# Query parts stored unsplit, key/value weights taken up later, and norm steps issued further on

## The chip, the core and the metric

The kernel runs on one core of one Trainium2 chip. The metric is the device time of one execution in microseconds (us): a median over runs, here 2845.11 us of 3 runs (2842.18 to 2846.28). Five engines work side by side, each through its own list of instructions in order: PE multiplies matrices and writes to PSUM (8 banks here, one tile `ps` each), DVE (VectorE) and ACT (ScalarE) do elementwise work, POOL (GpSimd) does some more of it, and SP issues nearly all DMA transfers. An instruction that waits holds up all that stands behind it on its engine.

## The reference, cut to what matters

One step of a diffusion backbone with two layers and 1152 tokens (1024 latent ones, 128 of context), 1024 features wide. Layer 0 mixes tokens with a gated recurrence, layer 1 with latent attention; each is followed by an MLP with a hidden width of 4096, and every sublayer starts with an RMS norm whose result is scaled and shifted by values worked out from a conditioning vector.

```python
for l in range(DEPTH):
    sh1, sc1, g1, sh2, sc2, g2 = adaln_params(c, ada_w[l], ada_b[l])
    h = modulate(rms_norm(xs, norm_mix[l]), sh1, sc1)
    if l % N_MIXERS == 0:
        out, _ = rglru_block(h, ...)
    else:
        q_nope, q_pe, ckv, kpe = mla_project(h, ...)     # 8 heads, 128 + 64 query rows each
        q_pe = apply_rope(q_pe, ...)
        k_nope, v = mla_kv(ckv, w_ukv)                   # keys, values of each head
        out = block_attention(q_nope, q_pe, k_nope, kpe, v) @ mla_w_o[j]
    xs = xs + g1[:, None, :] * out
    h = modulate(rms_norm(xs, norm_mlp[l]), sh2, sc2)
    xs = xs + g2[:, None, :] * sq_relu_mlp(h, mlp_w1[l], mlp_w2[l])
y_sample = rms_norm(xs, final_norm)
```

## The kernel before, in words

**Layout.** Features lie on the 128 partitions, tokens along the free axis, in three chunks of 384 tokens (`c` = 0, 1, 2; the last has 256 latent and 128 context tokens, so its elementwise steps come in pairs of 256 and 128). A product of 1024 features is 8 blocks of 128, for each of which `mm3` issues three matmuls of 384 columns, since each operand is held as a rounded high part and the low rest (`hi`, `lo`): hi·hi, hi·lo, lo·hi (L120, L123, L124). `split` (L138, L139) makes the two parts: an ACT cast writes `hi`, a DVE subtraction writes `lo`.

**Weights.** They come as a stream of 181 pieces of 128x1024. `prefetch` issues each one's DMA to `raw` (two buffers), an ACT cast to `whi` (L93) and a subtraction to `wlo` (L95, on POOL for all but the first pieces). `done(i)` says that piece i is used up and takes up the pieces three or four further on. With each piece, `prefetch` also issues `ada_rate` rows of the weights that make layer 1's scales and shifts: a DMA (L152) and two DVE dot products of 1024 elements (L144).

**Products and drains.** `group` goes through the chunks and in each through the output tiles m; after the matmuls of a tile it calls `drain`, which reads the PSUM bank. In `out_proj` (after the token mixer) and in the last of the eight groups of `mlp`, the drain adds the scaled product to the residual `X` (L297, DVE), and `sq_acc` squares the row on ACT (L221, L225) and adds the square to one of two sums per chunk (L227): even rows on DVE, odd rows on POOL.

**Norms.** When a chunk's last tile is out, `group` puts the generator `norm_mod(c)` on a list. After each tile `tick` takes 0.49 per block off its countdown, and when it is used up the generator goes on to its next `yield`. So `yield 2.9` means: one tile of 8 blocks (24 matmuls) further on, or two tiles of 4 blocks. The first part, `rstd`, sums over the partitions with six small matmuls against ones (L235, they wait for both sums) and works out the inverse root in 12 DVE steps on 128x3 values, `sv`, `st` and `sy` (L242 to L256). The second part, `spread`, transposes `sy` on PE (L263), and `modulate` makes the next products' operands `hhi`, `hlo` from it, 8 rows of 384 with a DVE, an ACT and a DVE step each (L283, L287, L288).

**Queries.** In `mla`, `qnope` splits each finished query tile from PSUM into `qn` and stores both parts to the DRAM tensor `qn_d` (L853), four heads at a time: 12 stores of 768 KB. The rotary parts `qpe` go through DMA swaps (L719, L720) and are stored to `qp_d` (L840). `attention` then loads three tiles of 576 KB per head (L882), makes values and keys of the first heads (`gen_v`, L909 to L911; `gen_k`) and starts on the scores. Before it the pools of `mla` are released, so tiles of `attention` lie where the query tiles lay and wait for these to be stored.

**Order.** The order in the code isn't the order on the engines: when the kernel is built, a scheduler takes the instructions of each stretch of code and orders each engine's list by its own model. Only instructions marked with `keep_in_program_order` keep their place.

## Time and profile before

| | |
|---|---|
| median of 3 runs | 2845.11 us (2842.18 to 2846.28) |
| the profiled execution | 2843.63 us, its span 2841.9 us |
| busy: PE, DVE, ACT, POOL | 97%, 49%, 41%, 17% of the span |
| granted TensorE clock, mean | 0.987 of full speed |
| gate outputs of `out_proj` and norms after the recurrence | about 440 to 512 us |
| last MLP group of layer 0 and its norms | about 1255 to 1335 us |
| queries, first values and keys | about 1400 to 1514 us |
| attention | 1514 to 1960 us |
| norms after the attention's `out_proj` | about 1975 to 2040 us |

The 40 slices of the page show PE at nine tenths or more nearly everywhere. So the views to read are PE's waits in a stretch of time (engine, line, what was waited for: sum in us, times, longest), and the busy time by stretches, with the granted clock (PEclk).

### The profile page before, as it was taken

How to read it: one execution, taken by the hardware profiler on the slowest of the kernel's cores; microseconds unless marked ns; L12 is line 12 of the kernel's file. 1: busy time of each engine (PE TensorE's matmuls, PEld its weight loads, DVE VectorE, ACT ScalarE, POOL GpSimd, SP SyncE). 2: the span in 40 equal slices, each digit the busy share in tenths (PEclk: the TensorE clock that was granted, in tenths of full speed). 3: DMA queues.
4: the chain of work that ended last, by engine and by line, in shares of the span. 5: the costliest groups of instructions: out<-in, count | busy, mean ns of one | idle time of the engine just before them, and what ended most of it. 6: DMA issues, size and time to landing. Idle time of an engine off the chain costs nothing. (4 is left out here: it accounts for less than half of the span.)

```text
span 2841.9 us, 39879 instructions
## 1 busy us (share of the span) xinstructions
PE 2749.7 (97%) x16123; PEld 2679.4 (94%) x16123; DVE 1403.4 (49%) x2806; ACT 1158.3 (41%) x2194; POOL 483.1 (17%) x247
## 2 busy tenths in 40 slices
PE   6999998999999999998998999999999999999998
PEld 3878898999999999998997999999999999999998
DVE  7788967545444542245545666652632222223225
ACT  4677733331232233144336777762422312322232
POOL 1000033121121212122241000002221211212121
PEclk9999999999999999999998999999999999999999
DMA  6122242222232221112264121134010111101011
GB/s 254 45 89 93 71 180 72 67 82 97 67 104 67 92 80 45 45 52 90 66 196 171 48 82 59 54 113 148 30 60 30 52 38 38 52 30 60 30 45 67
DMA packets 79465, 224.93 MB, mean 79 GB/s; under 512 B 7856, under 2 KB 36336, under 8 KB 77616
## 3 DMA queue, kind: packets, MB, share of 16 engines
q1 hardware_dynamic: 78512, 219.23, 22.6%
q0 software_dynamic: 768, 3.15, 0.3%
q8 instruction: 127, 2.08, 0.3%
q14 instruction: 58, 0.48, 0.1%
HBM read 186.52 MB, written 33.20 MB: 77 GB/s over the span
## 5 line engine op out<-in xcount | busy, mean ns | idle before, releaser
L95 POOL TENSOR_TENSOR wlo<-raw,whi 128x1024 fp32r<-128x1024 f32 x161 | 396.1, 2461 | 2009.0 <-ACT whi L93 1976.9
L120 PE MATMUL ps<-hhi,whi 128*128 128x384 f32 x2088 | 701.9, 338 | 3.6 <-ACT hhi L287 3.6
L123 PE MATMUL ps<-hlo,whi 128*128 128x384 f32 x2088 | 703.2, 337 | 0.0
L124 PE MATMUL ps<-hhi,wlo 128*128 128x384 f32 x2088 | 702.5, 337 | 0.4 <-DVE wlo L95 0.4
L93 ACT CAST whi<-raw 128x1024 fp32r<-128x1024 f32 x181 | 190.3, 1052 | 875.7 <-PE ps L123 729.8
L297 DVE SCALAR_TENSOR_TENSOR X<-ps,mod,X 128x256 f32<-128x256 f32 (+1 forms) x576 | 281.2, 513 | 493.5 <-PE ps L124 453.6
L120 PE MATMUL ps<-hid,whi 128*128 128x384 f32 x1536 | 516.3, 336 | 0.0
L123 PE MATMUL ps<-hid,whi 128*128 128x384 f32 x1536 | 515.5, 336 | 0.0
L124 PE MATMUL ps<-hid,wlo 128*128 128x384 f32 x1536 | 515.4, 336 | 0.0
L120 PEld LDWEIGHTS ps<-hhi,whi 128*128 128x128 f32 x2088 | 393.8, 189 | 12.1 <-ACT hhi L287 4.0
L123 PEld LDWEIGHTS ps<-hlo,whi 128*128 128x128 f32 x2088 | 394.2, 189 | 5.6 <-issue 5.2
L124 PEld LDWEIGHTS ps<-hhi,wlo 128*128 128x128 f32 x2088 | 394.2, 189 | 1.0 <-DVE wlo L95 1.0
L139 DVE TENSOR_TENSOR hid<-cell,hid 128x384 fp32r<-128x384 f32 x192 | 141.7, 742 | 491.7 <-ACT hid L138 491.6
L120 PEld LDWEIGHTS ps<-hid,whi 128*128 128x128 f32 x1536 | 288.9, 188 | 0.0
L123 PEld LDWEIGHTS ps<-hid,whi 128*128 128x128 f32 x1536 | 288.8, 188 | 0.0
L124 PEld LDWEIGHTS ps<-hid,wlo 128*128 128x128 f32 x1536 | 288.7, 188 | 0.0
L352 ACT ACTIVATE cell<-ps 128x384 f32<-128x384 f32 x192 | 93.6, 489 | 305.6 <-PE ps L124 305.6
L144 DVE SCALAR_TENSOR_TENSOR junk<-raw,cb 128x1024 bf16<-128x1024 f32 x56 | 99.7, 1781 | 106.7 <-DMA raw<-ada_wt 106.7
L947 ACT ACTIVATE p<-ps,nm 128x384 f32<-128x384 f32 (+1 forms) x200 | 112.9, 577 | 38.0 <-DVE nm L942 38.0
L139 DVE TENSOR_TENSOR pt<-ps,pt 128x384 fp32r<-128x384 f32 (+1 forms) x200 | 106.5, 543 | 36.8 <-ACT pt L138 36.5
L932 DVE TENSOR_REDUCE mx<-ps 128x1 f32<-128x384 f32 (+1 forms) x200 | 107.9, 539 | 25.7 <-PE ps L931 25.0
L353 ACT ACTIVATE cell<-cell 128x384 f32<-128x384 f32 x192 | 100.6, 525 | 5.9
(188 smaller groups left out, 4084.6 us busy)
## 6 DMA issues: line engine op xcount, KB each, us to landing
raw<-wts SPq DMA_DIRECT2D x181, 512.0 KB, 3.3
raw<-ada_wt SPq DMA_DIRECT2D x56, 512.0 KB, 3.3
adaw<-ada_n SPq DMA_DIRECT2D x24, 512.0 KB, 4.1
qn_d<-qn SPq DMA_DIRECT2D x12, 768.0 KB, 5.3
q<-qn_d SPq DMA_DIRECT2D x16, 576.0 KB, 5.2
o_d<-o SPq DMA_DIRECT2D x64, 128.0 KB, 1.7
x<-xt SPq DMA_DIRECT2D x3, 1536.0 KB, 14.1
X<-xt SPq DMA_DIRECT2D x3, 1536.0 KB, 11.8
```

Source lines behind the costliest of these rows:

```text
L93: nc.scalar.copy(out=hi, in_=raw)
L95: eng.tensor_tensor(out=lo, in0=raw, in1=hi.bitcast(F32), op=ALU.subtract)
L120: mm = nc.tensor.matmul(ps, lhsT=w[0], rhs=h[0], start=first, stop=False)
L123: nc.tensor.matmul(ps, lhsT=w[0], rhs=h[1], start=False, stop=False)
L124: nc.tensor.matmul(ps, lhsT=w[1], rhs=h[0], start=False, stop=last)
L139: (lo_eng or nc.vector).tensor_tensor(out=lo, in0=src, in1=hi.bitcast(F32), op=ALU.subtract)
L144: self.nc.vector.scalar_tensor_tensor(out=w if cond else self.junk, in0=w, scalar=1.0, in1=self.cb[cond], op0=ALU.mult, op1=ALU.mult, accu ...
L297: self.nc.vector.scalar_tensor_tensor(out=self.X[c][:, m, a:b], in0=ps[:, a:b], scalar=self.mod[:, l, j, cond, m:m + 1], in1=self.X[c][:, ...
L352: nc.scalar.activation(out=r, in_=ps, func=AF.Relu)
L353: nc.scalar.activation(out=r, in_=r, func=AF.Square)
L932: nc.vector.tensor_reduce(out=mx[:, j:j + 1], in_=ps, axis=AX.X, op=ALU.max)
L947: nc.scalar.activation(out=p[:, j * CH:j * CH + w], in_=ps, func=AF.Exp, scale=SCALE, bias=nm[:, 1:2], accum_out=sm[:, j:j + 1],)
```

## The change

1. **Norms.** In `norm_mod` the two countdowns become 4.0 and 5.0 (2.9 each before). For tiles of 8 blocks that is two tiles and two more; for tiles of 4 blocks three and three more. The final norm (`after` in `second_half`) keeps 2.9 and 2.9.
2. **Sums of squares.** Of the odd rows, the last one (i = 7) is added on DVE, not on POOL.
3. **Conditioning rows.** In `out_proj` the rate at which these rows are taken along with weights is set after the second `dense`, not before it.
4. **Queries.** `qnope` copies each tile from PSUM unsplit (one DVE copy); 6 stores of 768 KB take the place of 12. `attention` loads the unsplit tile into one new buffer `qraw` (two loads a head in place of three) and splits it into the `hi` and `lo` tiles there, a chunk of 384 at a time: for the first head after the first values and keys, for the others in steps 3 to 5 of the head before.
5. **Weights.** From the start of the query products, `prefetch` stops (`cap`) at the second of the four key/value pieces; the stop is lifted once the first values and keys and the first head's query parts are issued.

```diff
--- before.py
+++ after.py
@@ -61,6 +61,7 @@
         self.pending = []
         self.wpx = None
         self.pin = False
+        self.cap = 1 << 30
         self.ready = []
         self.used, self.oldest = set(), 0
         self.ada_i = 0
@@ -83,7 +84,7 @@
         nc = self.nc
         if self.wpx is None:
             upto = min(upto, len(RG_STREAM) + 3)
-        while self.piece_i < min(upto, self.I["wts"].shape[0]):
+        while self.piece_i < min(upto, self.cap, self.I["wts"].shape[0]):
             raw = self.wp.tile([128, 1024], F32, tag="raw", name="raw", bufs=2)
             nc.sync.dma_start(raw, self.I["wts"][self.piece_i])
             extra = self.wpx is not None and self.piece_i % 4 == 3
@@ -223,7 +224,7 @@
         else:
             s = self.cell()
             nc.scalar.activation(out=s, in_=src, func=AF.Square)
-            eng = nc.vector if key == 0 else nc.gpsimd
+            eng = nc.gpsimd if key and i < 6 else nc.vector
             eng.tensor_tensor(out=st[key], in0=st[key], in1=s, op=ALU.add)
 
     def rstd(self, st, width):
@@ -267,9 +268,9 @@
 
     def norm_mod(self, c, x, st, l, js, hi, lo):
         nc = self.nc
-        yield 2.9
+        yield 4.0
         y = self.rstd(st, D)
-        yield 2.9
+        yield 5.0
         self.modulate(c, x, self.spread(y), l, js, hi, lo)
 
     def modulate(self, c, x, r, l, js, hi, lo, ks=range(KT)):
@@ -391,7 +392,7 @@
             nc.vector.memset(self.ones, 1.0)
             self.mod = const.tile([128, 2, 6, 2, 8], F32, name="mod")
             self.xmid = nc.dram_tensor("xmid", [NCH, 128, 8, CH], F32).ap()
-            self.qn_d = nc.dram_tensor("qn_d", [2, HEADS, 128, T], F32).ap()
+            self.qn_d = nc.dram_tensor("qn_d", [HEADS, 128, T], F32).ap()
             self.o_d = [nc.dram_tensor(f"o_d{i}", [2, HEADS, 128, n], F32).ap() for i, n in ((0, 512), (1, T - 512))]
             self.qp_d = nc.dram_tensor("qp_d", [HEADS, 128, T], F32).ap()
             cp = self.alloc(name="cpool", bufs=9)
@@ -709,8 +710,8 @@
 
         rhs = lambda k, c: (Z[c][0][:, k], Z[c][1][:, k])
         self.dense(pi, range(4), rhs, drain)
+        self.dense(pi + 4, range(4, 8), rhs, drain, after)
         self.ada_rate = 1.0
-        self.dense(pi + 4, range(4, 8), rhs, drain, after)
         return H2
 
 
@@ -815,6 +816,7 @@
         pi += 7
 
         qt = {}
+        self.cap = pi + 8
 
         def qdrain(m, c, ps):
             if m < 4:
@@ -845,15 +847,13 @@
 
         def qnope(h, c, ps):
             cs = slice(c * CH, (c + 1) * CH)
-            if h % 4 == 0:
-                qt[c] = self.cbig(F32R, "qn")
-            self.split(qt[c][:, h % 4], qt[c][:, 4 + h % 4], ps)
+            if h == 0:
+                qt[c] = self.cbig(F32, "qn")
+            nc.vector.tensor_copy(out=qt[c][:, h], in_=ps)
             if h % 4 == 3:
-                for i in range(2):
-                    nc.sync.dma_start(
-                        self.qn_d[i, h - 3:h + 1, :, cs].rearrange("h p t -> p h t"),
-                        qt[c][:, 4 * i:4 * i + 4].bitcast(F32),
-                    )
+                nc.sync.dma_start(
+                    self.qn_d[h - 3:h + 1, :, cs].rearrange("h p t -> p h t"), qt[c][:, h - 3:h + 1]
+                )
 
         rhs = lambda k, c: (cq[c][:, k], cq[c][:, 4 + k])
         for ms in ((0, 4, 1, 5, 2, 6, 3, 7), range(8, 12)):
@@ -871,16 +871,17 @@
         nc = self.nc
 
 
-        pools = [self.alloc(name=n, bufs=1, reuse_waits="tile") for n in ("q0", "att", "k0", "attv")]
-        q0, at, k0, av = pools
+        pools = [self.alloc(name=n, bufs=1, reuse_waits="tile") for n in ("q0", "att", "k0", "attv", "qraw")]
+        q0, at, k0, av, self.qraw = pools
         Q, K, V = {}, {}, {}
 
         def load_q(h):
-            Q[h] = []
-            for src in (self.qn_d[0, h], self.qn_d[1, h], self.qp_d[h]):
-                t = (at if h % 2 else q0).tile([128, T], F32R, tag="q", name="q", bufs=3)
-                nc.sync.dma_start(t.bitcast(F32), src)
-                Q[h].append(t)
+            hi, lo, pe = ((at if h % 2 else q0).tile([128, T], F32R, tag="q", name="q", bufs=3) for _ in range(3))
+            raw = self.qraw.tile([128, T], F32, name="qraw")
+            nc.sync.dma_start(raw, self.qn_d[h])
+            nc.sync.dma_start(pe.bitcast(F32), self.qp_d[h])
+            Q[h] = hi, lo, pe
+            return lambda cs: self.split(hi[:, cs], lo[:, cs], raw[:, cs])
 
         def gen_k(h):
             pool, n = (at, 2 * NK) if h % 2 else (k0, 8 * CH)
@@ -1016,10 +1017,13 @@
 
             return [lambda t=t: part(t) for t in range(nt)]
 
-        load_q(0)
+        qsplit = load_q(0)
         gen_v(0)
         gen_k(1)
         gen_k(0)
+        for c in range(NCH):
+            qsplit(slice(c * CH, (c + 1) * CH))
+        self.cap = 1 << 30
         self.done(p0)
         steps = [[(h, i)] for h in range(HEADS) for i in range(7)]
         for h in reversed(range(HEADS)):
@@ -1030,7 +1034,9 @@
             if s < len(steps):
                 h, i = steps[s][-1]
                 if i == 1 and h + 1 < HEADS:
-                    load_q(h + 1)
+                    qsplit = load_q(h + 1)
+                if 3 <= i <= 5 and h + 1 < HEADS:
+                    qsplit(slice((i - 3) * CH, (i - 2) * CH))
                 if i == 5 and 0 < h < HEADS - 1:
                     gen_k(h + 1)
                     if h % 2 == 0:
```

In the listings, lines of the changed kernel are one higher than before in the norms (L228 is L227 of before), and some more further down (L833, L854).

**DVE, the inverse root of chunk 1 after the first `out_proj`** (`sy_3754` before, `sy_3782` now; L144 are conditioning rows). Before:

```order
L246 TENSOR_SCALAR st_3755<-sv_3753 128x3 [waits DVE_49]
L144 SCALAR_TENSOR_TENSOR junk_2955,mod_73<-raw_3742,cb_2952 128x1024 [waits DMAHW3_49]
L249 TENSOR_SCALAR sy_3754<-st_3755 128x3 [waits DVE_49]
L144 SCALAR_TENSOR_TENSOR raw_3742,mod_73<-raw_3742,cb_2952 128x1024 [waits DMAHW0_49,DVE_49,Pool_49]
L254 SCALAR_TENSOR_TENSOR st_3755<-sy_3754,sv_3753 128x3 [waits DVE_49]
L255 TENSOR_TENSOR st_3755<-st_3755,sy_3754 128x3 [waits DVE_49]
L256 SCALAR_TENSOR_TENSOR sy_3754<-st_3755,sy_3754 128x3 [waits DVE_49]
L254 SCALAR_TENSOR_TENSOR st_3755<-sy_3754,sv_3753 128x3 [waits DVE_49]
L255 TENSOR_TENSOR st_3755<-st_3755,sy_3754 128x3 [waits DVE_49]
L297 SCALAR_TENSOR_TENSOR X_2966<-ps_3768,mod_73,X_2966 128x256 [waits PE_49]
L256 SCALAR_TENSOR_TENSOR sy_3754<-st_3755,sy_3754 128x3 [waits DVE_49]
L297 SCALAR_TENSOR_TENSOR X_2966<-ps_3768,mod_73,X_2966 128x128
```

Now:

```order
L247 TENSOR_SCALAR st_3783<-sv_3781 128x3 [waits DVE_49]
L250 TENSOR_SCALAR sy_3782<-st_3783 128x3 [waits DVE_49]
L255 SCALAR_TENSOR_TENSOR st_3783<-sy_3782,sv_3781 128x3 [waits DVE_49]
L256 TENSOR_TENSOR st_3783<-st_3783,sy_3782 128x3 [waits DVE_49]
L298 SCALAR_TENSOR_TENSOR X_2966<-ps_3796,mod_73,X_2966 128x256 [waits PE_49]
L257 SCALAR_TENSOR_TENSOR sy_3782<-st_3783,sy_3782 128x3 [waits DVE_49]
L298 SCALAR_TENSOR_TENSOR X_2966<-ps_3796,mod_73,X_2966 128x128
L255 SCALAR_TENSOR_TENSOR st_3783<-sy_3782,sv_3781 128x3 [waits DVE_49]
L256 TENSOR_TENSOR st_3783<-st_3783,sy_3782 128x3 [waits DVE_49]
L257 SCALAR_TENSOR_TENSOR sy_3782<-st_3783,sy_3782 128x3 [waits DVE_49]
L255 SCALAR_TENSOR_TENSOR st_3783<-sy_3782,sv_3781 128x3 [waits DVE_49]
L228 TENSOR_TENSOR acc_3278<-acc_3278,cell_3823 128x384 [waits Activation_49,Pool_49]
```

The two dot products of 1024 elements are gone from the chain; a sum of squares (L228) stands in it at each end, and the residual step (L298) for the product that runs meanwhile stays in it. On PE, 24 matmuls lay between this chunk's last L235 and its L263; now 48 do.

**DVE, the inverse root of chunk 1 at the end of layer 0's MLP** (`X_2966` is the residual of chunk 2, whose tiles PE computes meanwhile). Before:

```order
L254 SCALAR_TENSOR_TENSOR st_10239<-sy_10238,sv_10237 128x3 [waits DVE_49]
L297 SCALAR_TENSOR_TENSOR X_2966<-ps_10252,mod_73,X_2966 128x128
L255 TENSOR_TENSOR st_10239<-st_10239,sy_10238 128x3 [waits DVE_49]
L256 SCALAR_TENSOR_TENSOR sy_10238<-st_10239,sy_10238 128x3 [waits DVE_49]
L254 SCALAR_TENSOR_TENSOR st_10239<-sy_10238,sv_10237 128x3 [waits DVE_49]
L255 TENSOR_TENSOR st_10239<-st_10239,sy_10238 128x3 [waits DVE_49]
L256 SCALAR_TENSOR_TENSOR sy_10238<-st_10239,sy_10238 128x3 [waits DVE_49]
L297 SCALAR_TENSOR_TENSOR X_2966<-ps_10276,mod_73,X_2966 128x256 [waits PE_49]
L254 SCALAR_TENSOR_TENSOR st_10239<-sy_10238,sv_10237 128x3 [waits DVE_49]
L297 SCALAR_TENSOR_TENSOR X_2966<-ps_10276,mod_73,X_2966 128x128
L255 TENSOR_TENSOR st_10239<-st_10239,sy_10238 128x3 [waits DVE_49]
L256 SCALAR_TENSOR_TENSOR sy_10238<-st_10239,sy_10238 128x3 [waits DVE_49]
```

Now:

```order
L256 TENSOR_TENSOR st_10263<-st_10263,sy_10262 128x3 [waits DVE_49]
L228 TENSOR_TENSOR acc_10184<-acc_10184,cell_10291 128x384 [waits Activation_49]
L257 SCALAR_TENSOR_TENSOR sy_10262<-st_10263,sy_10262 128x3 [waits DVE_49]
L298 SCALAR_TENSOR_TENSOR X_2966<-ps_10318,mod_73,X_2966 128x256 [waits PE_49]
L255 SCALAR_TENSOR_TENSOR st_10263<-sy_10262,sv_10261 128x3 [waits DVE_49]
L298 SCALAR_TENSOR_TENSOR X_2966<-ps_10318,mod_73,X_2966 128x128
L256 TENSOR_TENSOR st_10263<-st_10263,sy_10262 128x3 [waits DVE_49]
L257 SCALAR_TENSOR_TENSOR sy_10262<-st_10263,sy_10262 128x3 [waits DVE_49]
L255 SCALAR_TENSOR_TENSOR st_10263<-sy_10262,sv_10261 128x3 [waits DVE_49]
L256 TENSOR_TENSOR st_10263<-st_10263,sy_10262 128x3 [waits DVE_49]
L228 TENSOR_TENSOR acc_10184<-acc_10184,cell_10333 128x384 [waits Activation_49]
L257 SCALAR_TENSOR_TENSOR sy_10262<-st_10263,sy_10262 128x3 [waits DVE_49]
```

Before, the last steps of the root stood behind the residual of one tile (`ps_10276`); now they stand behind that of a later one (`ps_10318`) and behind the sum of its squares (`cell_10333`), which ACT makes from the same residual. On PE the scheduler has put one of this chunk's six L235 ahead and the other five 13 matmuls further on, so that 23 matmuls lie between the last of them and L264, as many as before; for the chunks 0 and 2 it is 36 and 48 (before 24 and 24).

**ACT and SP at the start of the attention.** `raw_12075` before and `raw_12269` now hold the third of the four key/value pieces, `raw_12275` the fourth. ACT before:

```order
L138 CAST qn_12057<-ps_12081 128x384 [waits PE_49]
L138 CAST qn_12057<-ps_12096 128x384 [waits PE_49]
L93 CAST whi_12077<-raw_12075 128x1024 [waits DMAHW6_49]
L138 CAST v_12139<-ps_12141 128x256 [waits DMAHW4_49,DMAHW5_49,DMAHW3_49,PE_49]
L138 CAST v_12139<-ps_12150 128x256 [waits PE_49]
```

ACT now:

```order
L139 CAST qpe_11725<-cell_11848 128x384 [waits DVE_49,Activation_49]
L94 CAST whi_12271<-raw_12269 128x1024 [waits DMAHW4_49,PE_49]
L94 CAST whi_12277<-raw_12275 128x1024 [waits DMAHW5_49,PE_49]
L139 CAST v_12097<-ps_12099 128x256 [waits DMAHW0_49,DMAHW3_49,DVE_49,PE_49]
L139 CAST v_12097<-ps_12108 128x256 [waits PE_49]
```

In both, weight casts stand ahead of the first cast of values `v`; there is one before, and there are two now. The first cast of values also waits for DMAs: its tile lies where query tiles lay. SP before:

```order
L853 DMA qn_d<-qn_11919 128x4x384 [waits DMAHW6_49]
L853 DMA qn_d<-qn_11919 128x4x384 [waits DMAHW7_49]
L840 DMA qp_d<-qpe_11735 64x4x384 [waits Activation_49]
L840 DMA qp_d<-qpe_11735 64x4x384 [waits DVE_49]
L840 DMA qp_d<-qpe_11735 64x4x384 [waits DMAHW2_49]
L840 DMA qp_d<-qpe_11735 64x4x384 [waits DMAHW3_49]
L853 DMA qn_d<-qn_11994 128x4x384 [waits DMAHW4_49]
L853 DMA qn_d<-qn_11994 128x4x384 [waits DMAHW5_49]
L88 DMA raw_12075<-wts 128x1024 [waits DMAHW6_49]
L853 DMA qn_d<-qn_12057 128x4x384 [waits DMAHW7_49,Activation_49]
```

SP now:

```order
L720 DMA cell_11867<-cell_11848 64x256 [waits DMAHW6_49,DMAHW2_49,DMAHW7_49,DVE_49,Activation_49]
L721 DMA cell_11867<-cell_11848 64x256 [waits DMAHW3_49]
L89 DMA raw_12269<-wts 128x1024 [waits DMAHW4_49]
L89 DMA raw_12275<-wts 128x1024 [waits DMAHW5_49]
L854 DMA qn_d<-qn_11588 128x4x384 [waits DVE_49]
L842 DMA qp_d<-qpe_11725 64x4x384 [waits Activation_49]
L842 DMA qp_d<-qpe_11725 64x4x384 [waits DMAHW0_49,DVE_49]
L842 DMA qp_d<-qpe_11725 64x4x384 [waits DMAHW1_49]
L842 DMA qp_d<-qpe_11725 64x4x384 [waits DMAHW2_49]
L854 DMA qn_d<-qn_11749 128x4x384 [waits DMAHW3_49,DVE_49]
L881 DMA qraw_12094<-qn_d 128x1152 [waits DMAHW4_49,Pool_49]
L882 DMA q_12093<-qp_d 128x1152 [waits DMAHW5_49,DMAHW7_49,DMAHW0_49,PE_49]
```

The DMAs of the two pieces now stand ahead of the last three groups of query stores; before, the third piece's stood behind two of them and the fourth's behind all. The last query store now (`qn_11749`, behind four of `qp_d`) is the one that the first cast of values waits for.

## The prediction

> **What bounds the kernel now.** PE does, and not by little: the page's first part has
>
> ```profile
> PE 2749.7 (97%) x16123; PEld 2679.4 (94%) x16123; DVE 1403.4 (49%) x2806; ACT 1158.3 (41%) x2194; POOL 483.1 (17%) x247
> ```
>
> The span is 2841.9 us, so PE idles 92 us in it, and no matmul of a dense product is taken away by the change. What it can win is in PE's stalls, and in what the clock loses after them. I read PE's waits next, in the four stretches that the change touches: 455 to 500, 1255 to 1335, 1975 to 2040 and 1400 to 1530 us, in this order:
>
> ```profile
> PE ps L263 <- DVE sy L256: 6.4, 1, 6.4
> PE ps L235 <- POOL acc L227: 1.9, 2, 1.5
> ...
> PE ps L263 <- DVE sy L256: 3.9, 1, 3.9
> PE ps L235 <- DVE acc L227: 2.6, 2, 1.8
> PE ps L235 <- POOL acc L227: 0.9, 2, 0.7
> ...
> PE ps L263 <- DVE sy L256: 3.9, 1, 3.9
> PE ps L235 <- POOL acc L227: 1.4, 2, 1.0
> ...
> PE ps L909 <- DVE v L139: 15.4, 1, 15.4
> PE ps L120 <- ACT cell L831: 1.2, 1, 1.2
> ```
>
> So the norms at the three places stall PE by 8.3, 7.4 and 5.3 us: for the sums (L235), more for the inverse root (L263). The attention's start stalls it by 15.4 us. Stretches chosen so that PE is busy all through show what follows a stall:
>
> ```profile
> 474.20:482.00 7.80, 7.80 (x30) 7.80 (x31) 6.00 (x11) 1.11 (x2) 0.00 (x0) 0.62 0.34 122
> 493.00:499.00 6.00, 6.00 (x31) 5.96 (x32) 3.72 (x16) 1.00 (x4) 0.00 (x0) 0.72 0.26 87
> 1292.40:1298.00 5.60, 5.60 (x24) 5.60 (x25) 3.78 (x7) 2.98 (x6) 0.44 (x1) 0.70 0.00 1
> 1312.00:1318.00 6.00, 6.00 (x28) 5.98 (x28) 1.95 (x12) 0.53 (x1) 0.00 (x0) 0.72 0.58 190
> 2009.40:2014.00 4.60, 4.60 (x19) 4.60 (x20) 4.24 (x10) 2.37 (x4) 0.00 (x0) 0.63 0.32 114
> 2026.00:2032.00 6.00, 6.00 (x27) 5.99 (x28) 2.75 (x14) 0.79 (x2) 0.00 (x0) 0.72 0.01 3
> 1486.90:1502.40 15.50, 0.07 (x2) 0.02 (x1) 0.49 (x2) 1.84 (x5) 0.72 (x1) 0.62 0.98 294
> 1502.40:1510.00 7.60, 7.60 (x38) 7.60 (x39) 4.13 (x12) 4.11 (x13) 4.05 (x2) 0.66 0.95 360
> ```
>
> The third number from the right is the granted clock. Width times what is missing from 1 gives the clock lost: 3.0 + 1.7 at the first place, 1.7 + 1.7 at the second, 1.7 + 1.7 at the third. The chain of waits has the matmuls of such a stretch and those just after it:
>
> ```profile
> 2029.51 0.32 PE ps L123
> ...
> 2030.25 0.18 PE ps L123
> ```
>
> 0.32 us is not quite twice 0.18 (0.174 over long runs), so of the lost clock some nine tenths are lost time: 4.2, 3.1 and 3.1 us.
>
> **Why the root is late.** Its 12 small steps take 3.1 us when nothing disturbs them and 7.8 at 2001 us:
>
> ```profile
> 494.39 0.16 DVE L242 TENSOR_SCALAR sv<-ps 128x3 f32<-128x3 f32 x1 [0.46 <-PE ps L235]
> ...
> 497.36 0.16 DVE L256 SCALAR_TENSOR_TENSOR sy<-st,sy 128x3 f32<-128x3 f32 x1
> ```
> ```profile
> 2001.34 0.15 DVE L242 TENSOR_SCALAR sv<-ps 128x3 f32<-128x3 f32 x1
> 2001.52 2.10 DVE L246 TENSOR_SCALAR st<-sv 128x3 int32<-128x3 int32 x1
> ...
> 2006.50 2.29 DVE L254 SCALAR_TENSOR_TENSOR st<-sy,sv 128x3 f32<-128x3 f32 x1
> ...
> 2009.01 0.16 DVE L256 SCALAR_TENSOR_TENSOR sy<-st,sy 128x3 f32<-128x3 f32 x1
> ```
> ```profile
> 2001.19 2.40 POOL L95 TENSOR_TENSOR wlo<-raw,whi 128x1024 fp32r<-128x1024 f32 x1 [1.42 <-ACT whi L93]
> ```
>
> The step of 2.10 us ends as POOL's weight subtraction ends; a step of this size otherwise takes 0.16. [...] The 24 matmuls that cover the root are worth 24 x 0.174 = 4.2 us.
>
> **Terms of the sum,** against the profiled execution's 2843.63 us.
>
> *Norms after the first out_proj.* The cover becomes 48 x 0.174 = 8.35 us. The worst root here lasted from 463.67 to 474.02, 10.4 us, but had two conditioning dots in it, of 1.21 each:
>
> ```profile
> 465.87 1.21 DVE L144 SCALAR_TENSOR_TENSOR junk<-raw,cb 128x1024 bf16<-128x1024 f32 x1
> ...
> 475.08 0.62 DVE L283 SCALAR_TENSOR_TENSOR cell<-X,mod,ps 128x384 f32<-128x384 f32 x1 [1.06 <-PE ps L263]
> ...
> 488.54 1.67 DVE L288 SCALAR_TENSOR_TENSOR hlo<-cell,mod,hhi 128x384 fp32r<-128x384 f32 x3
> ```
>
> Without them 8.0 us: just covered, though two sums of squares now stand in it. L235 comes one tile later too, so the sums are there. Of 8.3 + 4.2 = 12.5 I leave 0.8 for roots that meet POOL twice: **−11.7**. What is late next is the modulation: by the order of PE, 78 matmuls (13.6 us) now lie between L263 and the first that needs `hhi`. The last rows above show its eight rows take 15.1 us with dots in between; the eighth is needed 21 matmuls (3.7 us) after the first, at 17.2, so it is hidden by 2 us or more; without cover it would cost up to the 13.6.
>
> The conditioning rows go to the MLP's end: two dots a row, four rows, 8 x 1.21 = 9.7 us of DVE and four DMAs on SP, among 750 us in which DVE is half idle: 0.
>
> *Norms at the end of layer 0's MLP.* Chunks 0 and 2 get 36 and 48 matmuls; their stalls are for sums (2.6 + 0.9), which come 12 matmuls (2.1 us) later. Chunk 1, which had the 3.9, keeps its distance of 23 matmuls. Its root waits for the residual of a tile which ends right as L263 is due, then for its square on ACT and the sum: X 0.5 + 0.35, square 0.5, sum 0.55, last step 0.16, gives 2.1, with hand-overs 2.5; 4 if POOL cuts in. Taken 3.0 with half of the clock's 1.7: 7.4 + 3.1 − 3.0 − 0.8 = **−6.7** (bounds −4 to −9).
>
> *Norms after the second out_proj.* As the first, without dots: 7.8 us against 8.35; of 5.3 + 3.1 I leave 0.4: **−8.0**.
>
> *The attention's start.* PE fills its 8 banks with values, until 1486.95, and then waits for ACT:
>
> ```profile
> 1502.38 0.58 PE L909 MATMUL ps<-whi,ckv 128*128 128x256 f32 x1 [15.43 <-DVE v L139]
> ```
> ```profile
> 1500.56 1.04 ACT L93 CAST whi<-raw 128x1024 fp32r<-128x1024 f32 x1 [15.65 <-DMA raw<-wts]
> 1501.51 1.74 ACT L138 CAST v<-ps 128x256 fp32r<-128x256 f32 x6
> ```
> ```profile
> 1484.17 4.79 SPq L840 DMA_DIRECT2D qp_d<-qpe  x4
> 1489.01 3.76 SPq L853 DMA_DIRECT2D qn_d<-qn  x2
> 1492.81 1.57 SPq L88 DMA_DIRECT2D raw<-wts  x1
> ```
>
> The value casts could run from 1485 on, but stand behind a weight cast whose DMA is queued behind query stores, with the DMA engines 98% busy at 294 GB/s (row above). Now both late pieces are issued before these stores, so that their casts should be over by then; but the first value cast waits for the last query store. Moved between the last swap and what ACT waits for: before, two stores of 768 KB, four of 384, two of 768 and a piece of 512, 5.24 MB; now two pieces, one store, four and one, 4.19 MB. 1.05 MB at 294 GB/s are 3.6 us, and the cast of 1.04 us falls out: 4.6. A store reports later than a load (5.3 us against 3.3 at the median of the DMA table), and I take **−4**: the stall falls to 11. Bounds: −1, if the stores are slower in this order, and −8, if half the queue is gone before.
>
> *Splitting in the attention.* The 24 casts and subtractions move there:
>
> ```profile
> 1514.00:1960.00 446.00, 441.72 (x3108) 436.15 (x3107) 274.33 (x786) 315.25 (x785) 23.34 (x13) 1.00 0.26 89
> ...
> L139 DVE TENSOR_TENSOR qn<-ps,qn x24: 544/549/558, 1408.6 to 1485.1; 128x384 fp32r<-128x384 f32 x24
> L138 ACT CAST qn<-ps x24: 469/484/531, 1406.9 to 1484.4; 128x384 fp32r<-128x384 f32 x24
> ```
>
> ACT gets 24 x 0.48 = 11.6 us on 315 of 446, DVE 24 x 0.55 = 13.2 on 274. PE has 4 us of idle time there and the softmax chain some slack; exposed **+1** (0 to 4; all of it would be 25). [...]
>
> *Small ones.* The wait for `cell` (1.2) goes when the casts of `qn` leave ACT, and the last sum of squares before the final norm is quicker on DVE by some half us: **−1.0**. At the start of the kernel PE waits for loads, nothing.
>
> Sum: −11.7 − 6.7 − 8.0 − 4 + 1 − 1 = −30.4, so 2813.2 for the profiled execution. That lay 1.5 under the median of the runs, so **2814.7** as a median.
>
> **Rivals.** (a) *The wait at the attention's start goes altogether.* For it: the weights no longer stand in ACT's way. Against: the order has the value cast wait for the last store. The stall of 15.4 and the slow clock after it, 7.6 x 0.34 = 2.6, would give 18 in place of 4: 2801. (b) *The roots stay exposed,* because POOL's subtractions, which come with each weight piece, fall into the longer window as well, and DVE's other work with them. For it: 2.10 and 2.29 in one root. Against: 7.8 and 8.0 are the worst sums, and 8.35 covers them. Half of the norms' 26.4 lost: 2828. (c) *Query splits stall every head*: `qraw` is one buffer, so a head's load can't start until the last is split. If the load is issued only when it is needed, each of 7 heads waits for it and a cast and subtraction:
>
> ```profile
> q<-qn_d SPq DMA_DIRECT2D x16, 576.0 KB, 5.2
> ```
>
> 7 x (5.2 + 0.5 + 0.55) = 43.8 in place of 1: 2857, slower than before. It decides if the load is less than 6 us ahead of its cast. Against: a head is 446 / 8 = 56 us long, the load comes at its second step of seven and the split at the fourth, some 16 us later. (d) *The order undoes the change:* the scheduler has put both late weight casts ahead of the values, against the words of the edit; if their DMAs land late after all, the start wins nothing: 2819.
>
> [...]
>
> **How the numbers follow.** Forecast (with d, whose time lies in its range) 0.65, (a) 0.10, (b) 0.18, (c) 0.04, else 0.03. The range goes from (a) past (b), 2801 to 2834: below it a part of (a), above it (c) and losses that I don't see. What a measurement can tell from no change is 0.2%, 5.7 us. Faster: all but (c) and half of the rest, and a little of (b) for stalls that merely move: 0.91; same 0.05; slower 0.04.
>
> **What would show it.** Right: no wait of L264 for `sy` above 1 us in the out_proj stretches, and the granted clock there 0.95 or more; one of 2 to 4 us at the MLP's end; the wait of the value matmul at 10 to 12 us, ended through a store; the attention's 446 us unchanged within 3. Wrong: waits of L264 of 3 us or more after out_proj, waits of PE's `hhi` matmuls (the modulation late), or a `q` split as what PE waits for once per head.

## The result and the profile after

The changed kernel takes 2830.32 us (median of 5 runs), before 2845.11: a ratio of 0.995, 95% interval 0.9934 to 0.9966. So it is faster, by 14.8 us, where the forecast said 30.4; the time lies within the range, at a little under half of the forecast gain. In a second session, e1 below, it was 2832.52 against 2844.24, ratio 0.9961 (0.9946 to 0.9975). The median counts one execution of 8126.54 us, far from the other four (2830.08 to 2832.69), and since it was the one that was profiled, the trace read here is that of e1.

The first matmul that reads each operand marks the stages, so the traces can be laid side by side (us; e8 is an experiment below; the forecast's 1.0 for small things is shared out over two rows):

| stage, to the first matmul of the next | before | forecast | changed (e1) | e8 |
|---|---|---|---|---|
| start, recurrent layer | 361.7 | 0 | 365.4 (+3.7) | 361.2 (-0.5) |
| first out_proj and its norms, to the MLP's hidden rows | 175.0 | -11.7 | 168.1 (-6.9) | 162.6 (-12.4) |
| rest of layer 0's MLP, norms, low-rank projection | 864.5 | -6.7 | 862.3 (-2.2) | 852.9 (-11.6) |
| query products | 79.5 | -0.5 | 80.0 (+0.5) | 79.2 (-0.3) |
| first values and keys | 33.1 | -4 | 28.2 (-4.9) | 27.7 (-5.4) |
| attention | 391.4 | +1 | 394.2 (+2.8) | 394.3 (+2.9) |
| second out_proj to the end | 936.7 | -8.5 | 934.4 (-2.3) | 927.7 (-9.0) |
| span | 2841.9 | -30.4 | 2832.6 (-9.3) | 2805.6 (-36.3) |

Stages differ by up to 2 us between traces where nothing was changed: e3, which leaves the norms as they were, has 173.1 and 866.1 in the second and third row. The attention's start came as forecast. The three norm places brought 11.4 us with the final norm's part in it, not 26.9, and the start lost 3.7. PE's waits in the four stretches of before, after the change (455 to 500, 1255 to 1335, 1960 to 2030, 1390 to 1520 us; engine, line, what was waited for: sum, times, longest):

```profile
PE ps L264 <- DVE sy L257: 4.9, 1, 4.9
...
PE ps L264 <- DVE sy L257: 3.5, 1, 3.5
PE ps L236 <- DVE acc L228: 1.4, 1, 1.4
...
PE ps L264 <- DVE sy L257: 5.0, 1, 5.0
...
PE ps L910 <- DVE v L140: 10.7, 1, 10.7
PE ps L984 <- ACT p L969: 4.1, 1, 4.1
PE ps L121 <- ACT cell L833: 1.1, 2, 0.7
```

The waits for sums are gone after both out_proj, and a single wait for a root is left at each place. But it is 4.95 us long after both out_proj, although 48 matmuls now cover the root there. The root of chunk 1 shows why. Before, DVE began with it (`sv`) right after its sums:

```profile
462.16 1.28 PE L235 MATMUL ps<-ones,acc 128*128 128x2 f32 x10 [0.44 <-POOL acc L227]
...
463.67 0.15 DVE L242 TENSOR_SCALAR sv<-ps 128x3 f32<-128x3 f32 x1
```

PE, DVE and POOL of the changed kernel around 470 us (start, duration, engine, line, operation):

```profile
468.82 1.39 PE L236 MATMUL ps<-ones,acc 128*128 128x2 f32 x12
...
483.93 0.90 PE L264 MATMUL ps<-ident,sy 128*128 128x128 f32 x3 [4.95 <-DVE sy L257]
```
```profile
468.24 5.88 DVE L289 SCALAR_TENSOR_TENSOR hlo<-cell,mod,hhi 128x384 fp32r<-128x384 f32 x3
474.05 1.13 DVE L284 SCALAR_TENSOR_TENSOR cell<-X,mod,ps 128x384 f32<-128x384 f32 x2
475.10 1.38 DVE L298 SCALAR_TENSOR_TENSOR X<-ps,mod,X 128x256 f32<-128x256 f32 x4
476.40 1.90 DVE L289 SCALAR_TENSOR_TENSOR hlo<-cell,mod,hhi 128x384 fp32r<-128x384 f32 x2
478.22 0.15 DVE L243 TENSOR_SCALAR sv<-ps 128x3 f32<-128x3 f32 x1
478.29 2.63 DVE L228 TENSOR_TENSOR acc<-acc,cell 128x384 f32<-128x384 f32 x1
...
483.71 0.16 DVE L257 SCALAR_TENSOR_TENSOR sy<-st,sy 128x3 f32<-128x3 f32 x1
```
```profile
467.36 2.39 POOL L96 TENSOR_TENSOR wlo<-raw,whi 128x1024 fp32r<-128x1024 f32 x1 [3.66 <-ACT whi L94]
469.99 2.43 POOL L96 TENSOR_TENSOR wlo<-raw,whi 128x1024 fp32r<-128x1024 f32 x1 [0.24 <-ACT whi L94]
472.39 1.32 POOL L228 TENSOR_TENSOR acc<-acc,cell 128x384 f32<-128x384 f32 x1
```

PE has the sums at 470.2. DVE begins with the root at 478.22, 8 us later, for until then it does chunk 0's modulation, which is drawn out by three POOL operations in a row (three subtractions in 5.88 us, 1.7 in other places). The root itself then takes 5.6 us. Busy time in two stretches tells the same of the engine as a whole, the changed kernel's here (span, then PE, PEld, DVE, ACT and POOL, PEclk, DMA):

```profile
440.00:460.00 20.00, 20.00 (x121) 20.00 (x121) 7.89 (x21) 3.04 (x6) 2.29 (x2) 1.00 0.00 1
460.00:484.00 24.00, 19.05 (x114) 18.38 (x113) 23.16 (x39) 12.04 (x20) 12.19 (x6) 0.99 0.28 88
```

The kernel before, over the first of them:

```profile
440.00:460.00 20.00, 19.88 (x120) 19.56 (x119) 15.92 (x34) 8.18 (x14) 3.86 (x3) 1.00 0.00 1
```

DVE's 15.92 us of work fell to 7.89 in the first 20 us, since chunk 0's spread, and with it its modulation, now comes 48 matmuls later; then DVE is busy for 23.16 of 24 us. Some 9 of these are no work of its own but time by which its operations are drawn out beside POOL, as an estimate from rows like those above (5.88 us for 1.7, 2.63 and 2.44 for two sums of 0.55, 1.90 for 1.1). Work was moved from where DVE had room to where, with POOL in its way, it had none.

### The profile page after: what moved, and what is told of

The parts are those of the page before. It is cut to its first block, busy times and chain, and to the rows that moved or that the text cites. A ratio compares the mean times of both kernels' runs of the same rounds, so it can differ in the third digit from the quotient of the medians.

```text
span 8124.8 us, 39857 instructions
## 1 busy us (share of the span) xinstructions
PE 8089.1 (100%) x16123; PEld 6011.4 (74%) x16123; DVE 1430.2 (18%) x2845; ACT 1188.1 (15%) x2194; POOL 458.2 (6%) x232
## 4 chain that ended last, share of the span: by engine, by line
PE 100%; DVE 0%; ACT 0%; DMA 0%; issue 0%; SPq 0%; DVEq 0%; ACTq 0%
PE ps L121 28%; PE ps L124 28%; PE ps L125 28%; PE ps L166 3%; PE ps L984 2%; PE ps L928 1%; PE ps L1008 1%; PE ps L1010 1%; PE ps L930 1%; PE ps L931 1%; PE ps L932 1%; PE ps L1009 1%; PE ps L929 1%; PE ps L236 1%; PE ps L910 0%; PE ps L912 0%
## 5 line engine op out<-in xcount | busy, mean ns | idle before, releaser
L121 PE MATMUL ps<-hhi,whi 128*128 128x384 f32 x2088 | 1654.0, 795 | 3.0 <-ACT hhi L288 3.0
L125 PE MATMUL ps<-hhi,wlo 128*128 128x384 f32 x2088 | 1655.4, 793 | 0.0
L124 PE MATMUL ps<-hlo,whi 128*128 128x384 f32 x2088 | 1655.0, 793 | 0.0
L121 PE MATMUL ps<-hid,whi 128*128 128x384 f32 x1536 | 1185.2, 772 | 0.0
L124 PE MATMUL ps<-hid,whi 128*128 128x384 f32 x1536 | 1184.7, 771 | 0.0
L125 PE MATMUL ps<-hid,wlo 128*128 128x384 f32 x1536 | 1184.2, 771 | 0.0
L121 PEld LDWEIGHTS ps<-hhi,whi 128*128 128x128 f32 x2088 | 833.6, 399 | 317.2 <-issue 256.9
L124 PEld LDWEIGHTS ps<-hlo,whi 128*128 128x128 f32 x2088 | 830.8, 398 | 308.1 <-issue 255.3
L125 PEld LDWEIGHTS ps<-hhi,wlo 128*128 128x128 f32 x2088 | 837.6, 401 | 291.0 <-issue 241.0
L121 PEld LDWEIGHTS ps<-hid,whi 128*128 128x128 f32 x1536 | 601.9, 392 | 200.2 <-issue 166.1
L125 PEld LDWEIGHTS ps<-hid,wlo 128*128 128x128 f32 x1536 | 599.3, 390 | 203.6 <-issue 169.0
L124 PEld LDWEIGHTS ps<-hid,whi 128*128 128x128 f32 x1536 | 598.1, 389 | 200.0 <-issue 165.7
L298 DVE SCALAR_TENSOR_TENSOR X<-ps,mod,X 128x256 f32<-128x256 f32 (+1 forms) x576 | 285.9, 515 | 2577.1 <-PE ps L125 2558.2
```

The lines of the kernel that those rows point to most:

```text
L121: mm = nc.tensor.matmul(ps, lhsT=w[0], rhs=h[0], start=first, stop=False)
L124: nc.tensor.matmul(ps, lhsT=w[0], rhs=h[1], start=False, stop=False)
L125: nc.tensor.matmul(ps, lhsT=w[1], rhs=h[0], start=False, stop=last)
L298: self.nc.vector.scalar_tensor_tensor(out=self.X[c][:, m, a:b], in0=ps[:, a:b], scalar=self.mod[:, l, j, cond, m:m + 1], in1=self.X[c][:, ...
```

## The experiments

Two theories stood against each other first, that the norms are right and the queries dear (A), or that the roots stay exposed (B). e1 is the changed kernel itself:

> The changed kernel itself, for a trace at the usual clock. Its median came out 14.8 us under the median of before, where 30.4 were forecast. The forecast's terms were -11.7, -6.7 and -8.0 us for the norms, -4 for the attention's start, +1 for the splits, -1 for small things. Theory A (norms right, queries dearer): PE's waits for L264 and L236 are gone but for some 3 us at the end of layer 0's MLP, and some 16 us more than forecast are lost between the query products and the end of the attention: the value wait is 15 us or more and PE waits for splits. Theory B (roots stay exposed): L264 still waits 3 us or more at two places at least, and the attention's start and the 446 us behind it are as forecast.

Measured 2832.52 us, with the waits shown above: theory B in its outcome. The next two take the change apart. e2 has only the norm part (this diff and the next ones show only the lines that matter, with remarks after `#`):

```diff
-        yield 2.9            # norm_mod, ahead of rstd
+        yield 4.0
-        yield 2.9            # ahead of spread
+        yield 5.0
-            eng = nc.vector if key == 0 else nc.gpsimd
+            eng = nc.gpsimd if key and i < 6 else nc.vector
-        self.ada_rate = 1.0  # ahead of the second dense; now behind it
```

> Before, with the norm steps further on, the last odd square on DVE and the conditioning rows after the second out_proj group; queries and weights as before. Theory A: 26 to 28 us faster than before (11.7 + 6.7 + 8.0 and half a us at the end). Theory B: 11 to 16 us faster.

Measured 2835.28 us against 2844.24, ratio 0.9965 (0.9954 to 0.9977): 9.0 us, under what B gave and far under A. e3 has only the rest of the change:

> The change without its norm part: queries stored unsplit and split in the attention, weights held back, norms as before. Theory A: 8 to 14 us slower than before, since the norms' 26 became 15 in the whole. Theory B: 2 to 6 us faster (-4 at the start, +1 for the splits, -1 for the query products).

Measured 2840.13, ratio 0.9988 (0.9978 to 0.9997): 4.1 us faster, as B said. Theory A falls: the queries cost nothing that the norms would have had to pay for.

The runs from e4 on come from three more sessions, in which the kernel before took 2845.48 (e4 to e7), 2843.13 (e8 to e10) and 2845.74 us (e11, e12). The changed kernel was not run again in them, so a difference from its 2832.52 us, or between runs of two sessions, is good to 1 to 3 us.

That left the question of why the roots stay exposed: because POOL draws out the root's own steps on DVE (theory L, in the expectations "POOL's lock": before, one such step took 2.10 us beside a subtraction of 2.40 on POOL, where others took 0.16), or because other work stands ahead of the root on DVE (theory Q). First a smaller matter, the sum of squares that the change moved from POOL to DVE. e4:

```diff
-            eng = nc.gpsimd if key and i < 6 else nc.vector
+            eng = nc.gpsimd if key else nc.vector
```

> The changed kernel with the last odd square added on POOL again. In the changed kernel the first dense products start 3.7 us later than before (365.4 against 361.7 us), with PE waiting 2.86 us for a sum at 60.4 us where it waited 0.69. Theory: four sums in a row on DVE are the cause, since the kernel's start has chunk sums that follow each other directly; 3 to 4 us come back there, and the two waits of 4.95 us for the roots of chunk 1 shrink by up to 2.6 (the sum that stands in the root), so 2822 to 2829 as a median. Rival (the countdowns move the start): nothing comes back there.

Measured 2831.31; by the trace the dense products start at 362.1 us again. PE's wait for the sum there, before, in the changed kernel, in e4:

```profile
59.68 1.50 PE L235 MATMUL ps<-ones,acc 128*128 128x2 f32 x12 [0.69 <-DVE acc L227]
```
```profile
60.41 2.72 PE L236 MATMUL ps<-ones,acc 128*128 128x2 f32 x12 [2.86 <-DVE acc L228]
```
```profile
59.20 1.50 PE L236 MATMUL ps<-ones,acc 128*128 128x2 f32 x12 [1.46 <-DVE acc L228]
```

So the start's 3.7 us are the moved sum in the main: it makes four in a row on DVE, with PE waiting for the last. 3.3 came back. Over all traces the dense products start at 362.7 to 365.9 us with the sum on DVE (seven kernels) and at 361.2 to 363.3 with it on POOL (six), some 2.5 us apart on the mean. The waits for the two roots grew a little instead of shrinking (5.2 us each), so of that expectation's second half nothing held. It had named the wrong sum. The one of 2.63 us inside the root is another row's and is still there in e4 (at 475.84 us, again 2.63 long).

e5 takes work from DVE in the modulation after both out_proj and gives ACT something in its place:

```diff
         nc.scalar.activation(out=hi, in_=t, func=AF.Identity, bias=sh, scale=1.0)
+        if getattr(self, "no_lo", False):       # norms after out_proj
+            nc.scalar.activation(out=lo, in_=t, func=AF.Copy, scale=0.0)
+            return
         nc.vector.scalar_tensor_tensor(
```

> The changed kernel without the low parts of the norms' results after both out_proj: ACT writes zeros in their place, so DVE has 8 subtractions of 0.6 us fewer per chunk and none that POOL can hold up there. Theory Q (queue): the root of chunk 1 is late because chunk 0's modulation stands ahead of it on DVE (sv began 8.0 us after its six matmuls had ended); with a third of that work gone both waits of 4.95 us fall under 1.5, the time by 8 to 13 us against the changed kernel. Theory L (POOL's lock on the root's own steps): sv comes at once, but the root still takes 5.5 us and more; waits of 3 us or more remain.

Measured 2817.21 us, 15.3 under the changed kernel, a little more than expected; in its trace PE's waits in 455 to 500 and in 1955 to 2030 us are an empty list. DVE begins the root 0.04 us after the sums (470.50, against 470.46), and though POOL still draws out three of the root's own steps (0.92, 0.87 and 2.32 us) and the root takes 6.0 us, as theory L had it, PE does not wait: theory Q. The wait at the MLP's end, where the low parts are made on DVE as ever, is still there (5.0 us).

e6 takes POOL's weight subtractions away at the same place (its sums stay), at the price of more work for DVE:

```diff
-            eng = nc.vector if self.piece_i < len(RG_STREAM) else nc.gpsimd
+            eng = nc.vector if self.piece_i < len(RG_STREAM) or getattr(self, "wlo_dve", False) else nc.gpsimd
```

with `wlo_dve` set during `out_proj`.

> The changed kernel with the weight subtractions of the pieces taken up during both out_proj on DVE (1.2 us each) in place of POOL (2.4 us each): no lock by weights there, but more work on DVE. If the lock is what makes the modulation long (three subtractions took 5.9 us, 1.8 is usual), the waits of 4.95 us fall to 1 to 3. If DVE is full without it too, they stay at 4 or grow.

Measured 2830.31. The waits, first and second out_proj:

```profile
PE ps L264 <- DVE sy L257: 3.6, 1, 3.6
...
PE ps L264 <- DVE sy L257: 3.8, 1, 3.8
```

This lies between the two expectations, and it does not measure POOL's part: two of the subtractions that DVE took over, 3.2 us in all, stand between the sums and the root, which begins 7.05 us after its sums. In the changed kernel, beside POOL's work, three subtractions ahead of the root took 4.2 us more (5.88 against 1.7) and a sum inside it 2.1 more (2.63 against 0.55). That is 6.3 us, more than the wait of 4.95. So as an estimate the wait takes both, chunk 0's late modulation and what POOL adds to it, and taking away either one would end it. No run has POOL's work there away with nothing in its place; that the order alone is enough, e8 and e11 show. e7 keeps all work and changes its order, so that the root stands ahead of the last three modulated rows:

```diff
-        self.modulate(c, x, self.spread(y), l, js, hi, lo)
+        r = self.spread(y)
+        if js != 3:          # not after out_proj
+            self.modulate(c, x, r, l, js, hi, lo)
+            return
+        self.modulate(c, x, r, l, js, hi, lo, ks=range(5))
+        yield 9.0
+        self.modulate(c, x, r, l, js, hi, lo, ks=range(5, KT))
```

> The changed kernel with the last three of a chunk's eight modulated rows issued two tiles later after both out_proj, so that the next chunk's root stands ahead of them on DVE. Theory Q: sv comes some 4 us earlier, the waits of 4.95 us fall to about 1, and the time by 5 to 10 us against the changed kernel, unless the MLP's first products wait for the three late rows (then PE waits for hhi, up to 4 us each). Theory L: the waits stay at 3 us or more.

Measured 2834.13. No root is waited for any more, and the same time is lost one step on:

```profile
482.31 0.69 PE L121 MATMUL ps<-hhi,whi 128*128 128x384 f32 x1 [4.78 <-ACT hhi L294]
```

4.78 us for the late rows, in place of 4.95 for the root. This is the case that the expectation named beside theory Q's gain. It says what bounds the place: not which of the two DVE does first, but how much it has to get through between chunk 0's spread and the matmuls that need the results.

So the spread has to come early for chunk 0, and late for chunk 1, whose root is the one that needs cover. e8 (`js` is 3 after out_proj and 0 for the other norms, the recurrent layer's first one among them, where `wpx` is None):

```diff
-        yield 4.0
+        first, second = (((2.9, 2.9), (2.9, 5.0), (4.0, 5.0)) if js
+                         else ((2.9, 2.9), (6.0, 7.0), (4.0, 5.0)))[c]
+        yield first
         y = self.rstd(st, D)
-        yield 5.0
+        yield second
-            eng = nc.gpsimd if key and i < 6 else nc.vector
+            eng = nc.gpsimd if key and (i < 6 or self.wpx is None) else nc.vector
```

> The changed kernel with countdowns by chunk: after both out_proj 2.9 and 2.9 for chunk 0, 2.9 and 5.0 for chunk 1, 4.0 and 5.0 for chunk 2; at the end of layer 0's MLP 2.9 and 2.9, 6.0 and 7.0, 4.0 and 5.0; the last odd square on POOL in the recurrent layer's first norm. Theory Q (DVE idles while chunk 0's root waits to be spread, and is then full: 3.0 of 20 us busy before, 23.2 of 24 after): with chunk 0 spread 24 matmuls earlier its modulation is over when chunk 1's root begins, and chunk 1's root has 48 matmuls of cover. Both waits of 4.95 us fall under 1, those of 1.4 and 3.5 at the MLP's end under 1 too, 3 us come back at the start: 2808 to 2816 as a median. Theory L (POOL's lock on the root itself): the waits after out_proj stay at 3 us or more, 2820 or more.

Measured 2807.2 us against 2843.13, ratio 0.9875 (0.986 to 0.989): 35.9 us faster than before and 25 faster than the change, the fastest of all. Its waits in 455 to 500 and 1955 to 2030 us (between 1250 and 1335 it has none), and DVE's load:

```profile
PE ps L236 <- DVE acc L228: 0.4, 1, 0.4
PE ps L264 <- DVE sy L257: 0.2, 1, 0.2
...
PE ps L236 <- DVE acc L228: 0.4, 1, 0.4
```
```profile
440.00:460.00 20.00, 19.88 (x120) 19.56 (x119) 16.02 (x33) 8.18 (x14) 4.50 (x3) 1.00 0.00 1
460.00:484.00 24.00, 23.37 (x139) 22.96 (x138) 22.13 (x41) 10.70 (x18) 9.38 (x6) 1.00 0.26 88
```

DVE is busy for 16.0 and 22.1 us in the two stretches, where the changed kernel had 7.9 and 23.2. (The 3.0 of 20 us in the expectation is ACT's column, misread; DVE's was 7.89.)

e9 tries the other stall that is left, at the attention's start, by laying the first values elsewhere:

```diff
-        pools = [... for n in ("q0", "att", "k0", "attv", "qraw")]
+        pools = [... for n in ("q0", "k0", "att", "attv", "qraw")]
-        nc.scalar.copy(out=hi, in_=src)
+        cast = nc.scalar.copy(out=hi, in_=src)
+        if pin:              # first values, keys and query parts
+            self.tc.keep_in_program_order(cast)
```

> The changed kernel with two pools of the attention in another order (k0 ahead of att), so that the first values no longer lie where the last stored query tile lies, and with the first casts of values, keys and query parts pinned in the code's order. The forecast named the wait of the first value cast for the last query store as what keeps the stall at 11 us (10.73 came). If that is so, the values are cast as soon as they are there, the keys wait for stores that end some 3 us earlier, and the scores start 5 to 9 us earlier; the time falls by 4 to 9 us against the changed kernel. If the DMA queue as a whole is the bound (the first head's queries land at the same time as before), PE waits for keys or queries in place of values and less than 3 us are won.

Measured 2843.34 us, 10.8 slower than the changed kernel. In the changed kernel the value casts waited for a store; in e9 they run at once, and then keys and queries wait, and a transfer after the attention is late:

```profile
1492.04 2.31 ACT L139 CAST v<-ps 128x256 fp32r<-128x256 f32 x8 [10.25 <-DMA qn_d<-qn]
```
```profile
1477.73 2.98 ACT L139 CAST v<-ps 128x256 fp32r<-128x256 f32 x10
1485.82 1.42 ACT L139 CAST k<-ps 128x320 fp32r<-128x320 f32 x4 [5.11 <-DMA qp_d<-qpe]
1488.44 1.08 ACT L139 CAST k<-ps 128x320 fp32r<-128x320 f32 x3 [1.20 <-DMA qn_d<-qn]
1492.55 1.04 ACT L94 CAST whi<-raw 128x1024 fp32r<-128x1024 f32 x1 [3.03 <-DMA raw<-wts]
...
1494.38 0.69 PE L930 MATMUL ps<-k,q 128*128 128x384 f32 x1 [7.04 <-ACT q L139]
...
1903.50 0.69 PE L124 MATMUL ps<-oz,whi 128*128 128x384 f32 x1 [13.13 <-DMA oz<-o_d]
```

The stage from the first value product to the scores took 25.1 us in place of 28.2: the store wait was real, and behind it the DMA queue as a whole is the bound, for the waits end one after another as it drains. The trace of e3 agrees: there the values are cast at once (1486.81), and PE waited 4.8 us for values and then for keys; the stages of values, keys and attention together took 420.4 us (424.5 before, 422.4 in e1). The 13.13 us at 1903 us are a price that nobody had on the list: POOL loads the operands of the second out_proj from 1893.5 us on, where in e1 it began at 1846.2. The other order of the pools is the likely reason, but it was not run without the pins. e10 has e8's and e9's edits together:

> The two edits of the countdowns by chunk and of the pools and pins together. They meet at different places, so their gains should add: under theory Q and the store wait 2801 to 2811 as a median; under the others 2818 or more.

Measured 2821.68, ratio 0.9921 (0.9908 to 0.9933): 14.5 us over e8, so e9's loss comes with it and the sum that was expected of two gains falls.

Two runs take e8 apart. e11 undoes one thing of the change, the countdowns of chunk 0 after both out_proj:

```diff
-        yield 4.0
+        early = js == 3 and c == 0
+        yield 2.9 if early else 4.0
         y = self.rstd(st, D)
-        yield 5.0
+        yield 2.9 if early else 5.0
```

> The changed kernel with one thing undone: after both out_proj, chunk 0 alone has its countdowns of 2.9 and 2.9 again. Theory Q: the modulation of chunk 0 then ends some 8 us earlier against chunk 1's sums (four tiles earlier spread by 24 + 24 matmuls), so chunk 1's root begins as soon as its sums are there and both waits of 4.95 us fall under 1; 10 to 14 us faster than the changed kernel, nothing else moves. If chunk 1's own countdowns or the start matter more, less than 5 us come.

Measured 2816.85, ratio 0.9904 (0.9888 to 0.9921): 15.7 us faster than the changed kernel, more than expected (17.2 by the differences from before in either session), and PE's waits after both out_proj are gone. By the stages, the first out_proj's takes 161.4 us (168.1 in e1) and the last one 926.8 (934.4), 14.3 of the difference. DVE in its trace is idle until the sums come, and then begins the root:

```profile
469.49 0.16 DVE L243 TENSOR_SCALAR sv<-ps 128x3 f32<-128x3 f32 x1 [0.49 <-PE ps L236]
```

So the countdowns of one chunk, at two places, are what kept the forecast gain away there. e12 is e8 with the conditioning rows back in the second out_proj group:

> The kernel with countdowns by chunk (2807.2 us) with one thing more undone: the conditioning rows run again from before the second out_proj group, two dots of 1.21 us for each weight piece taken up there. The forecast counted 2.4 us for two dots in one root. With 48 matmuls of cover a root of 8 to 10 us is at the edge: 0 to 3 us of wait at the first out_proj, 0 to 5 us slower than 2807.2. Under theory Q the dots also delay the modulation, so the wait should come back, at 2 us or more.

Measured 2811.99, 4.8 over e8 (3.1 by the ratios to before, 0.9886 against 0.9875, whose intervals overlap), with the root's wait back in the first out_proj:

```profile
475.81 0.54 PE L264 MATMUL ps<-ident,sy 128*128 128x128 f32 x3 [2.84 <-DVE sy L257]
```

By the stages the first out_proj's takes 166.5 us (162.6 in e8). One of the two dots in the root took 3.28 us beside POOL. So moving the rows was worth some 3 to 4 us here, a little more than the two dots (2.4 us) that the forecast had counted.

## Why the forecast was right and wrong

**Norms after the out_proj (forecast -11.7 and -8.0).** The failing step is "just covered": the cover of 8.35 us was set against the root's own duration, 8.0, as though the root began when its sums were there. It began 8.0 us after them; the duration itself was put too high (5.6 us came). I had read which instructions stand inside the root on DVE, and not those ahead of its first; chunk 0's modulation stood there, because its spread was moved with the rest. The sentence "what is late next is the modulation" looked only to the matmul that needs it, where it was indeed hidden, and not to the engine that it shares with the next root. With chunk 0's countdowns undone alone (e11) the two stages brought 13.6 and 9.9, and with countdowns by chunk (e8) 12.4 and 9.0, against 11.7 and 8.5: the sizes of the terms were right, the condition was not.

**MLP's end (-6.7, bounds -4 to -9).** The wait for chunk 1's root was put at 3.0 and came as 3.45 (in the seven other traces with these countdowns, 3.3 to 5.0, so that the size fits so well is in part luck); the waits for sums were taken as gone, and one of 1.36 stayed. Of the clock I had taken half of 1.7 us to be left, and after the second wait alone 2.9 were lost in e1 (6.4 us at 0.54, in the last section). So -2.2, outside the bounds; over those eight traces it is -0.6 to -3.8. e8, with 48 matmuls and a later sum, got 11.6 from this stage.

**The start (0).** "At the start of the kernel PE waits for loads, nothing" is wrong: the moved sum cost 3.7 there in e1 (e4 gave 3.3 back; 2.5 on the mean of all traces). The term was put under small ones for the end only.

**The attention's start (-4, stall 11).** Right: the stall is 10.73, and ACT's cast at 1492.04 follows the landing of the last query store. The bound behind it is the DMA queue (e9 and e3), as the 1.05 MB in the working had it.

**Splitting in the attention (+1).** +2.8, within 0 to 4, but not by what the term meant. PE's first wait there rose from 3.0 to 4.1 us, and the granted clock fell after it (PEclk 0.63 and 0.52 in 1514 to 1518), which it had not done before (1.00 in 1523 to 1533); by an estimate from these numbers the two make some 2.6 of the 2.8. The first head's splits now stand beside its first scores, and one of their subtractions took 1.57 us (1505.93) in place of 0.56, beside a weight subtraction of POOL's (1504.68 to 1507.08): an overlap that the term had no part for. DVE got 11 us of work more (265.13 to 276.23 us over the stage, by the stretches below), ACT 8:

```profile
1513.80:1905.20 391.40, 387.12 (x2795) 381.56 (x2795) 265.13 (x766) 306.32 (x771) 12.78 (x8) 1.00 0.20 68
```
```profile
1504.00:1898.00 394.00, 388.63 (x2793) 382.58 (x2792) 276.23 (x787) 314.67 (x791) 12.73 (x8) 1.00 0.18 56
```

No split is waited for by PE within a head; rival (c) did not come.

**Rivals.** (b), half of the norms' gain lost, gave 2828, and 2830.32 came; and both things that it named were at work: POOL's subtractions and "DVE's other work with them". That the time agrees to 2 us is luck in part: it halved the norms' gain without a price for either, and did not see that they act ahead of the root, nor that the change itself had put chunk 0's modulation there. (a) and (d) did not come.

## What to carry to other kernels

When a step is moved later to give a wait more cover, look at what the same engine does for the next unit of work: an idle gap opened early is paid back where the engine is full, and mending the order there can bring the wait back under the next name (e7). Read the queue ahead of the first instruction of a chain, not only the chain. A delay that one unit needs may be wrong for its neighbour: here chunk 0 wanted its spread early and chunk 1 late, and countdowns by chunk, with one sum put back, gave 25 us over one countdown for all.

## What the runs showed of the hardware

The same stall of 4.95 us cost differently in clock at its two places. Busy stretches right after it, and the one after the MLP's 3.45 us:

```profile
484.00:490.00 6.00, 6.00 (x28) 6.00 (x29) 5.14 (x10) 3.03 (x6) 0.00 (x0) 0.74 0.00 0
1293.60:1300.00 6.40, 6.40 (x23) 6.40 (x24) 5.23 (x10) 3.66 (x7) 0.87 (x1) 0.54 0.00 1
2011.40:2018.00 6.60, 6.60 (x27) 6.60 (x28) 5.75 (x12) 3.63 (x7) 0.00 (x0) 0.63 0.01 2
```

The third number from the right is the granted clock. 6.0 x 0.26 = 1.6 us of clock after one, 6.6 x 0.37 = 2.4 after the other, and 6.4 x 0.46 = 2.9 after the shortest, which had a wait of 1.36 us some 10 us ahead of it. So the clock's part of a stall can't be taken in proportion to it, as I had done at the MLP's end. In the kernel before, it was 0.72 after waits of 1.49 and 0.99 us (493 to 499 and 2026 to 2032) and 1.00 after one of 2.97 (1523 to 1533). What else the cost depends on is not shown: no run here moved a stall alone.

DVE's subtractions in the modulation were drawn out while POOL worked: three of them took 5.88 us beside 467.36 to 473.71 on POOL, and 1.7 elsewhere. That this falls on the modulation, and reaches the root through the queue, was the part that I had not expected.
